# Attention's planned list begins with the last value group, holds the first output weights, and is planned anew (one Trainium2 core)

## The chip, the core and the metric

The kernel runs on one core of one Trainium2 chip. Five engines share the core's memory: TensorE (PE, matmuls; PEld are its weight loads), VectorE (DVE), ScalarE (ACT), GpSimd (POOL) and SyncE (SP, which issues the DMAs here). Each engine works off its own queue in order and waits at an instruction until what that instruction needs is there. The metric is the device time of one execution in microseconds (us); lower is better. Of the kernel before there are three runs, 1249.63 to 1252.88 us, median 1252.07 us.

## What is computed

One decoder layer on 1024 tokens of width 1024, in float32:

```python
h   = x * (1 + scale1) + shift1                  # modulation from c
q, k, v, u, iq, ik, iw = split(h @ w_in)         # 8 heads of 64; rope on q, k, iq, ik
score = sum_h iw_h * relu(iq_h . ik)             # the indexer, causal
keep the 256 highest scores of each query row; softmax attention over those alone
mixer = concat(attention, causal window pools of u) @ w_o
x = LayerNorm(alpha * x + gate1 * mixer)
x = LayerNorm(alpha * x + gate2 * SwiGLU(x * (1 + scale2) + shift2))
```

The choice of 256 keys a row is exact: the kernel searches a threshold for each row, bit by bit, and turns it into a mask that is added to the attention scores. Tokens are worked in eight tiles of 128 rows; tile i sees 128(i + 1) keys, so tiles 0 and 1 need no search.

## The kernel before, in words

**Matmuls.** A float32 operand is split into a high and a low part and multiplied in three passes (`SPLITS`), so a projection group of 128 tokens by 512 columns is 8 x 3 = 24 matmuls.

**Stages.** (1) Modulation and indexer projections. (2) Indexer scores. (3) Projection groups, the list `groups` (line 969): eight pooling groups, eight key groups, eight value groups, worked in the loop of lines 974 to 1021; actions that belong to a group are put off to a later slot with `at_`. Value group t is copied from its PSUM bank by `v_take` one slot later. (4) Attention, lines 1166 to 1392. (5) Output projection (`wo_*`) and the first LayerNorm, then the feed-forward part in a hand-made order, which the change does not touch.

**Threshold searches.** `bisect` (line 607) is a generator that yields one step at a time with the engine and an expected cost. There are streams for the tiles [3], [5, 4] (search passes on ACT, a `Sign` activation with a summed output), and [7, 6], [2] (on DVE; tile 2 drops the largest scores eight at a time, `drop_eights`, line 590). Each ends in `mask_steps`. During the projection groups, `fill` (line 727) slips a step in wherever the modelled queue has room. Line 975 appends to `hold` at the last value group: from there `fill` starts no step on ACT and none of a tile other than 7's stream.

**Attention's list.** Work is cut into 32 units (head pair pr, tile i), two of them making one output. A unit is a row of tasks, each with an engine, a cost and a rank: `s` scores on PE, `x` (mask, scale and row maximum, DVE), `e` exponentials (ACT), `r` reciprocal (DVE), `n` multiplication by it (POOL), `p` transposes (PE), `c` copies of these out of PSUM (ACT or DVE); then `o`, the product with the values (PE), `hi` (ACT) and `lo` (DVE). For each query tile below 6 there are `load` (SP), `turn` (PE transposes), `own` and `other` (ACT) and `low` (DVE) as well. PSUM banks are two rings (four small, two large). A list scheduler (lines 1356 to 1391) then repeats: it works out the earliest start of every task and search step that could go, takes all that could start within `SPAN` of the earliest, and emits the one of lowest rank (`PRIO`, for search steps `CHAIN_PRIO`; `V_BIAS` is added to the start of a copy on DVE). What it emits is the fixed program order on PE, DVE, ACT and POOL. So the costs decide only the order; the chip decides when each instruction runs.

**Before and after the list.** The last two groups' copies (`late` slots 24 and 25) come ahead of it. After it come, in the program, the output weights: `wo_load(k)` (DMA, then the gate row multiplied in on POOL) and `wo_split(k)` (high part on ACT, low part on DVE). These are not held in order, and the compiler's scheduler moves them up among the attention's instructions where it sees room. WO[0] and WO[1] lie where the rows of query tiles 7 and 6 lay; WO[2] to WO[7] lie where the keys lay. Three raw slots (`raw_slot`) take turns for query rows, output weights and pooled rows.

Of the kernel before, what the change touches and what calls it, by code (L numbers as in the profile page):

```python
# [18 lines left out]
ALU = mybir.AluOpType  # L19

P = 128
# [19 lines left out]
EAGER = 0  # L41
Q_LEAD = 40
CHAIN_LEAD = 1
V_BIAS = -0.075
SPAN = 0.106
PRIO = {'load': -387, 'turn': -49, 'own': -168, 'low': -13, 'other': -88, 's': 3, 'x': -36, 'e': 1, 'r': 152, 'n': -121, 'p': 12, 'c': 332, 'o': -134, 'hi': -115, 'lo': 145}
CHAIN_PRIO = {2: (500, 22.3), 3: (347, 6.4), 4: (-732, 10.2)}
AHEAD_SMALL = 2
NORM = 2
NORM_SMALL = 2  # L50
# [145 lines left out]
def decoder_layer_kernel(  # L196
# [375 lines left out]

    def mask_steps(i, T1, ng, eq, lt):
        n, sc, w = P * (i + 1), score(i), (i + 1) / 8
        yield "V", 1.7 * w + 0.1

        V.tensor_scalar(eq, sc, T1, None, ALU.is_equal)
        V.tensor_scalar(lt, sc, T1, float(TOPK - n), ALU.is_lt, ALU.add, accum_out=ng)
        V.tensor_scalar(ng, ng, -0.5, None, ALU.add)
        yield "V", 1.6 * w  # L580
        left = sc.bitcast(BF16)[:, 0:n]
        V.tensor_tensor_scan(left[:, ::-1], eq[:, ::-1], eq[:, ::-1], ng, ALU.add, ALU.bypass)
        V.tensor_scalar(left, left, 0.0, None, ALU.is_lt)
        yield "V", 1.8 * w
        V.tensor_tensor(eq, eq, left, ALU.mult)
        V.tensor_tensor(lt, lt, eq, ALU.max)
        V.tensor_scalar(sc, lt, NOT_TAKEN, None, ALU.mult)
        biased.add(i)

    def drop_eights(i, cols):  # L590

        n = P * (i + 1)
        neg = buf("X", 4800, n, "neg")
        m8, ng, T1 = cols[:, 0:8], cols[:, 8:9], cols[:, 9:10]
        yield "V", 0.5
        V.tensor_scalar(neg, score(i), -1.0, None, ALU.mult)
        for r in range((n - TOPK) // 8):
            yield "V", 1.0
            V.max(m8, neg)
            V.match_replace(neg, m8, neg, -3.4e38)  # L600
        yield "V", 0.7
        V.max(m8, neg)
        V.tensor_scalar(T1, m8[:, 0:1], -1.0, None, ALU.mult)
        halves = neg.bitcast(BF16)
        yield from mask_steps(i, T1, ng, halves[:, 0:n], halves[:, n : 2 * n])
# [365 lines left out]
    PAIRS = (0, 6, 8, 14, 16)  # L971
    held, pair = {}, None
    qr = {}
    for n_, (kind, a, b) in enumerate(groups):
        if n_ == len(groups) - 1:
            hold.append(1)
        if n_ == 17:
            qr.update((i, q_load(i)) for i in (7, 6))
        if n_ in (20, 21):
            at_(n_, lambda i=27 - n_: q_make(i, qr[i]))  # L980
        if n_ in PAIRS:
            pb = psB("pair")
# [12 lines left out]
        if n_ in (7, 8, 15, 16):  # L995
            for kp in ((0, 1) if n_ % 2 else (2, 3)):
                w_split(kp)
        nd = n_ + 2 if n_ in PAIRS else n_ + 1
        if kind == "u":
            at_(nd, lambda a=a, b=b, pp=pp: u_take(a, b, pp))  # L1000
            if b == 1:
                at_(nd + 1, lambda a=a: u_split(a))
                at_(nd + 1, lambda a=a: u_split2(a))
                at_(nd + POOL_AT, lambda a=a: u_pool(a))
        elif kind == "k":
            tr = n_ + (4 if n_ in PAIRS or n_ - 1 in PAIRS else 3)
            at_(nd, lambda a=a, pp=pp, tr=tr: take(a, pp, tr))
        else:
            at_(nd, lambda a=a, pp=pp: v_take(a, pp))
        if n_ == 20:  # L1010
            SP.dma_start(GR, gate_d[0].to_broadcast([P, 1024]))
        q_ = n_ - MOD_AT
        if 0 <= q_ < 9:
            if q_:
                mod_fin(q_ - 1)
            if q_ < 8:
                mod_half(2 * q_)
        for f in late.pop(n_, []):
            f()
        if 0 <= q_ < 8:  # L1020
            mod_half(2 * q_ + 1)
    last = len(groups)
    pinned.clear()


    stat = [buf("X", 8448, 128, "stat")]
# [6 lines left out]

    ptb = [[buf("H", (2 * s_ + e) * 2048, 2048, "pT").rearrange("p (j q) -> p j q", j=8) for e in (0, 1)] for s_ in (0, 1)]
    smr = buf("H", 8192, 6144, "sm")
    for s_ in (last, last + 1):
        for f in late.pop(s_, []):
            f()
    assert not late, late
    def cat_slot(g):  # L1040
        return WS[g]

# [79 lines left out]
    def wo_load(k):  # L1122
        wo_raw[k] = raw_slot()
        SP.dma_start(wo_raw[k], wo_in[k])
        G.tensor_tensor(wo_raw[k], wo_raw[k], GR, ALU.mult)

    def wo_split(k):
        split(WO[k], wo_raw[k], 1024)
# [10 lines left out]
    def pool_split(q):  # L1139
        r = pl_raw[q].rearrange("p (g t) -> p g t", t=256)  # L1140
        for hi, lo, src in ((PLT0[:, 0, q], PLT0[:, 1, q], r[:, 0]),
                            (PLT[:, ::-1, 0, q], PLT[:, ::-1, 1, q], r[:, 1:4])):
            A.activation(hi, src, AF.Copy)
            V.tensor_tensor(lo, src, f_(hi), ALU.subtract)

    class Task:

        def __init__(self, kind, q, cost, rank, emit, deps=(), slots="", late=0.0):
            self.q, self.cost, self.rank, self.emit, self.deps, self.slots, self.late = q, cost, rank + PRIO[kind], emit, deps, slots, late
            self.end, self.kind, self.masks = None, kind, ()  # L1150

    class Ring:

# [20 lines left out]
    sm_of, o = {}, 0  # L1174
    for u in units:
        n = P * (u[2] + 1)
        if n > 512:
# [6 lines left out]
    q_done, q_turns = {7: (), 6: ()}, []  # L1184
    masked = {0: 0.0, 1: 0.0}

    def q_rows(t, rank):
        hold_ = {}

# [22 lines left out]
                V.tensor_tensor(lv[64:128], pv[64:128], f_(qv[64:128, :, 1, :]), ALU.subtract)  # L1212

        l_ = task("load", "S", 0.1, rank, load, q_turns[-3:-2], late=4.0)
        t_ = task("turn", "T", 0.55, rank, turn, (l_,), "A", late=0.2)
        c0 = task("own", "A", 1.2, rank, lambda: copies(0), (t_,))
        lw = task("low", "V", 1.4, rank, lambda: copies(2), (c0,))
        c1 = task("other", "A", 1.2, rank, lambda: copies(1), (c0,))
        t_.readers = (c1, lw)
        t_.masks = {1: (3,), 0: (4, 5)}.get(t, ())  # L1220
        q_done[t] = (c1, lw)
        q_turns.append(t_)

    def unit(k):
# [18 lines left out]
        def n_(e):  # L1243
            G.tensor_scalar(sms[e], sms[e], cols["c"][:, 2 + e : 3 + e], 0.0, ALU.mult, ALU.add)

        s_t = task("s", "T", 0.2 + 0.0014 * n, 10 * k - EAGER, s_, q_done[i], "B" if n <= 512 else "BB", late=0.2)
        before = [t for w in where for t in sm_users.get(w, ())]
        xs = [task("x", "V", 0.08 + 0.00105 * n, 10 * k, lambda e=e: x_(e), [s_t] + before, late=0.12) for e in (0, 1)]
        for x in xs:
            x.masks = (i,)  # L1250
        s_t.readers = xs
# [4 lines left out]
        for e in (0, 1):  # L1256
            for j0 in range(0, i + 1, 4):
                m = min(4, i + 1 - j0)
                hold_ = {}

                def p_(e=e, j0=j0, m=m, hold_=hold_):
                    hold_["pt"] = pt = psA("pT")
                    for j in range(m):
                        T.transpose(pt[:, j * P : (j + 1) * P], sms[e][:, (j0 + j) * P : (j0 + j + 1) * P], ident)

# [9 lines left out]
                c = task("c", "AV", (0.09 + 0.11 * m, 0.09 + 0.13 * m), 10 * k + 3, c_, [p] + list(o_tasks[-2:-1]), late=0.1)  # L1275
                p.readers = (c,)
                ps.append(p)
                cs.append(c)
        for w in where:
            sm_users[w] = ps  # L1280
        return cs

    o_tasks = []
# [3 lines left out]
    for k in range(0, nu, 2):  # L1287
# [11 lines left out]
            ca = cat_slot(g)  # L1299
            V.tensor_tensor(ca[:, 1024 + pr * 256 : 1024 + (pr + 1) * 256], hold_["po"][:, 0:256], f_(ca[:, pr * 256 : (pr + 1) * 256]), ALU.subtract)  # L1300

        o_t = task("o", "T", 0.1 + 0.865 * (g + 1), 10 * k + 14, o_, cs, "A", late=0.3)
        h_t = task("hi", "A", 0.3, 10 * k + 15, hi_, (o_t,), late=0.1)
        l_t = task("lo", "V", 0.38, 10 * k + 16, lo_, (h_t,), late=0.1)
        o_t.readers = (l_t,)
# [1 line left out]
    class Chain:  # L1307
# [5 lines left out]
        def step(self):  # L1313
# [4 lines left out]
            self.cost = (0.95 if self.q == "A" else 1.08) * self.st[1][1]  # L1318
# [11 lines left out]
    def earliest(t, q):  # L1330
        at = clock[q]
        for d in t.deps:
            if d.end is None:
                return FAR
            at = max(at, d.end)
        for i in t.masks:
            if i not in masked:
                return FAR
# [23 lines left out]
    while todo or chains:  # L1362
# [15 lines left out]
        if q == "T":  # L1378
            cost += 0.15 * (kind[0] != t.kind)
            kind[0] = t.kind  # L1380
        if t.slots:
            t.got = rings[t.slots[0]].take(len(t.slots))
        t.emit(q) if len(t.q) > 1 else t.emit()
        clock[q] = at + cost
        t.end = at + cost + t.late
        todo.remove(t)
# [744 lines left out]
```

## Time and profile before

| | value |
|---|---|
| runs, median (range) | 1252.07 us (1249.63 to 1252.88) |
| profiled execution, its own time | 1250.99 us |
| span, first to last instruction | 1249.2 us |
| busy: PE / DVE / ACT / POOL | 1180.4 / 1002.0 / 656.0 / 709.3 us |
| mean granted TensorE clock | 0.981 |
| attention's list, first score matmul to last output matmul | about 333.7 to 472.3 us |

In the profile's answers a row of a timeline gives the start, the duration and the engine, then the tile written, the tiles read, the shape and the count of merged instructions; a bracket at its end gives the idle time of the engine ahead of it and what ended that. A row of the table by stretches gives, for each engine in turn (PE, PEld, DVE, ACT, POOL), the busy time and in brackets the number of instructions, then the granted TensorE clock (1.00 is full speed), the DMA share and GB/s. A row of groups gives total busy us, mean ns of one, and the idle time before them. All compute is emitted through one helper at line 183, so tiles are told apart by name: `s` scores, `sm` the weights of a unit, `pT` their transposes, `o` the output, `pj` a projection group, `qT` and `qab` a query tile turned and its copies, `vf` values, `keysA`, `junkB`, `colsA` the search of tile 3, `neg`, `colsE` that of tile 2, `raw` the raw slots, `wo` output weights and their product.

### The profile page before, as it was taken

To read this page: it belongs to the slowest core of one execution; us is meant where nothing else is said; L and a number is where in the kernel's file an instruction comes from. 1 tells how busy PE (TensorE), PEld (TensorE's weight loads), DVE (VectorE), ACT (ScalarE), POOL (GpSimd) and SP (SyncE) were. 2 spreads that over 40 slices of the span, in tenths; PEclk is the share of its full clock that TensorE was granted. 3 is DMA by queue.
4 is the path that set the end of the run, shared out by engine and by line. 5 is a ranking of instruction groups with operands and counts; after the bars stand their busy time and mean duration, and the time that the engine had idled before them with its cause. 6 is when DMAs were issued, how large, how long until landed. Compare 5 with 4: busy or idle time off the path is not lost.

```text
span 1249.2 us, 16310 instructions
## 1 busy us (share of the span) xinstructions
PE 1180.4 (94%) x5622; PEld 919.8 (74%) x5622; DVE 1002.0 (80%) x1772; ACT 656.0 (53%) x1330; POOL 709.3 (57%) x505
## 2 busy tenths in 40 slices
PE   8999989999888899997899999999999999999996
PEld 6756556687665568876778787877878787878775
DVE  6799997988989975686977878787777768687698
ACT  4667878787789683455343434333333333442521
POOL 0093484676034362286784838475665748486848
PEclk9999999999989899997999999999999999999998
DMA  9610167421101035001312111112102020213212
GB/s 349 251 49 11 47 242 280 154 70 60 43 1 35 34 134 174 39 9 34 102 34 68 34 68 34 68 34 67 68 34 72 32 99 23 81 34 101 68 51 118
DMA packets 32459, 103.40 MB, mean 83 GB/s; under 512 B 3572, under 2 KB 3572, under 8 KB 28792
## 3 DMA queue, kind: packets, MB, share of 16 engines
q1 hardware_dynamic: 32376, 102.36, 23.1%
q8 instruction: 44, 0.72, 0.2%
q14 instruction: 39, 0.32, 0.1%
HBM read 92.90 MB, written 9.45 MB: 82 GB/s over the span
## 4 chain that ended last, share of the span: by engine, by line
PE 38%; DVE 7%; POOL 5%; issue 2%; ACT 1%; DVEq 0%; POOLq 0%; ACTq 0%
PE gu L183 23%; PE dn L183 15%; DVE act_W L183 2%; DVE utmp_X L183 2%; POOL wraw_R L183 1%; POOL wblk_T L183 1%; POOL wraw_W L183 1%; POOL wblk_V L183 1%; DVE gtmp_V L183 1%; DVE wblk_T L183 1%; DVE hr_H L183 0%; POOL hr_H L183 0%; DVE stat_C L183 0%; DVE wblk_V L183 0%; DVE res_X L183 0%
## 5 line engine op out<-in xcount | busy, mean ns | idle before, releaser
L183 PE MATMUL gu<-hr_H,wblk_T 128*128 128x512 f32 (+1 forms) x924 | 216.9, 387 | 2.6 <-ACT gtmp_V L183 2.3
L183 PE MATMUL gu<-hr_H,wblk_V 128*128 128x512 f32 (+1 forms) x924 | 215.1, 384 | 2.4 <-ACT gtmp_V L183 1.7
L183 PEld LDWEIGHTS gu<-hr_H,wblk_T 128*128 128x128 f32 x924 | 171.7, 190 | 38.7 <-ACT gtmp_V L183 2.9
L183 PEld LDWEIGHTS gu<-hr_H,wblk_V 128*128 128x128 f32 x924 | 170.0, 188 | 38.6 <-ACT gtmp_V L183 2.2
L183 DVE TENSOR_TENSOR res_X<-res_X,dn 128x512 f32<-128x512 f32 (+1 forms) x253 | 158.5, 675 | 15.4 <-PE dn L183 15.3
L183 POOL TENSOR_TENSOR wraw_R<-wraw_R 128x512 f32<-128x512 f32 x64 | 93.9, 1475 | 45.8 <-DVE wblk_T L183 23.1
L183 POOL TENSOR_TENSOR wraw_W<-wraw_W 128x512 f32<-128x512 f32 x60 | 85.8, 1437 | 55.8 <-DVE wblk_V L183 27.4
L183 PE MATMUL pj<-ws_W,hT_H 128*128 128x512 f32 x456 | 115.7, 400 | 1.0 <-DVE ws_W L183 1.0
L183 POOL TENSOR_SCALAR sm_H<-sm_H,stat_X 128x1024 f32<-128x1024 f32 (+7 forms) x64 | 49.1, 783 | 96.9 <-DVE stat_X L183 83.0
L183 PEld LDWEIGHTS pj<-ws_W,hT_H 128*128 128x128 f32 x456 | 83.0, 188 | 24.9 <-issue 6.5
L183 PE MATMUL dn<-wblk_T,act_W 128*128 128x512 f32 x324 | 79.4, 393 | 1.9 <-POOL wblk_T L183 1.2
L183 PE MATMUL dn<-wblk_V,act_W 128*128 128x512 f32 x324 | 78.8, 392 | 1.1 <-POOL wblk_V L183 1.1
L183 DVE TENSOR_SCALAR_CACHE_REDUCE junk_X<-keysD_T,colsD_X 128x1024 int16<-128x1024 int16 (+1 forms) x64 | 79.4, 1268 | 0.2
L183 ACT ACTIVATE wblk_V<-wraw_R 128x512 fp32r<-128x512 f32 x56 | 35.2, 629 | 80.7 <-POOL wraw_R L183 69.1
L183 PEld LDWEIGHTS dn<-wblk_T,act_W 128*128 128x128 f32 x324 | 60.1, 188 | 17.4 <-POOL wblk_T L183 3.9
L183 ACT ACTIVATE wblk_V<-wraw_W 128x512 fp32r<-128x512 f32 x53 | 33.1, 628 | 75.9 <-POOL wraw_W L183 62.4
L183 PEld LDWEIGHTS dn<-wblk_V,act_W 128*128 128x128 f32 x324 | 60.2, 188 | 16.2 <-POOL wblk_V L183 3.9
L183 ACT ACTIVATE wblk_T<-wraw_W 128x512 fp32r<-128x512 f32 x56 | 35.0, 628 | 65.9 <-POOL wraw_W L183 53.8
L183 ACT ACTIVATE wblk_T<-wraw_R 128x512 fp32r<-128x512 f32 x52 | 32.5, 627 | 61.3 <-POOL wraw_R L183 51.3
L183 PE MATMUL pT<-const_C,sm_H 128*128 128x128 f32 x288 | 45.2, 299 | 15.7 <-POOL sm_H L183 8.2
L183 DVE SCALAR_TENSOR_TENSOR score_X<-relu_K,const_C,score_X 128x384 f32<-128x384 f32 (+5 forms) x42 | 54.1, 1289 | 5.0 <-ACT relu_K L183 1.3
L183 ACT ACTIVATE utmp_X<-gu 128x512 f32<-128x512 f32 x33 | 19.7, 598 | 73.0 <-PE gu L183 73.0
(301 smaller groups left out, 2717.4 us busy)
## 6 DMA issues: line engine op xcount, KB each, us to landing
mset_K<-in_wmr_dram SPq DMA_DIRECT2D x16, 1024.0 KB, 5.3
wm_K<-in_wma_dram SPq DMA_DIRECT2D x16, 512.0 KB, 10.2
wraw_R<-in_wg_dram SPq DMA_DIRECT2D x6, 1024.0 KB, 4.7
wraw_R<-in_wd_dram SPq DMA_DIRECT2D x12, 512.0 KB, 3.6
wraw_W<-in_wup_dram SPq DMA_DIRECT2D x12, 512.0 KB, 3.5
wraw_R<-in_wup_dram SPq DMA_DIRECT2D x10, 512.0 KB, 3.6
wraw_W<-in_wg_dram SPq DMA_DIRECT2D x5, 1024.0 KB, 4.8
wraw_W<-in_wd_dram SPq DMA_DIRECT2D x10, 512.0 KB, 3.5
```

The costliest lines, as they stand in the source:

```text
L183: ins_ = f(*a, **k)
```

## The change

1. The loop over `groups` leaves out the last value group. Its matmuls and the last two copies are tasks (`group`, `take`) of the list. What overwrites memory that this group reads waits for it: the query rows of tiles 5, 4 and 3, the rows `x` of every unit but the first, the first copies of a unit. The first unit gets rows of its own (`sm_first`), so it can run ahead of the group.
2. Nothing is put into `hold`, and the queues stay held in order from the groups into the list, SP too.
3. The output weights' first three loads and gate products and the first two splits are tasks of the list. Loads are issued in the order in which they were made (`behind`).
4. A one-column exponential is put at slot 22, so the table for exponentials is loaded there.
5. When the list expects PE to wait more than 0.5 us ahead of transposes, it puts spare transposes (0.55 of the gap less 0.5 us, 0.11 us each) into the bank first.
6. Costs of tasks are changed, some search steps get a separate cost for the list, and all ranks, `SPAN` and `V_BIAS` are new.

```diff
-V_BIAS = -0.075
-SPAN = 0.106
-PRIO = {'load': -387, 'turn': -49, 'own': -168, 'low': -13, 'other': -88, 's': 3, 'x': -36, 'e': 1, 'r': 152, 'n': -121, 'p': 12, 'c': 332, 'o': -134, 'hi': -115, 'lo': 145}
-CHAIN_PRIO = {2: (500, 22.3), 3: (347, 6.4), 4: (-732, 10.2)}
+V_BIAS = 0.15
+KEEP = 0.55
+SPAN = 0.15
+PRIO = {'load': 650, 'turn': 53, 'own': -1350, 'low': -687, 'other': 600, 's': -261, 'x': -1371, 'e': 71, 'r': -915, 'n': 1966, 'p': -227, 'c': 659, 'o': -951, 'hi': -1034, 'lo': 641, 'gate': -895, 'group': 863, 'take': 1269, 'whi': -1001, 'wlo': -635}
+CHAIN_PRIO = {2: (1157, 15.6), 3: (1224, 52.0), 4: (1044, 55.3)}
...
-        yield "V", 1.7 * w + 0.1
+        yield "V", 1.7 * w + 0.1, False, 1.7 * w + 0.5
...
-        yield "V", 1.6 * w
+        yield "V", 1.6 * w, False, 3.4 * w
...
-        yield "V", 1.8 * w
+        yield "V", 1.8 * w, False, 2.9 * w
...
-            yield "V", 1.0
+            yield "V", 1.24
...
-    for n_, (kind, a, b) in enumerate(groups):
-        if n_ == len(groups) - 1:
-            hold.append(1)
+    for n_, (kind, a, b) in enumerate(groups[:-1]):
...
+        if n_ == 22:
+            at_(n_, lambda: A.activation(colsE[:, 16:17], ident[:, 0:1], AF.Exp))
...
-    last = len(groups)
-    pinned.clear()
+    last = len(groups) - 1
...
-    for s_ in (last, last + 1):
-        for f in late.pop(s_, []):
-            f()
+    (take_22,) = late.pop(last)
...
+    sm_first = [buf("X", 5312, 1024, "sm"), buf("V", 7168, 1024, "sm")]
...
+    def group_23():
+        got["pp"] = psA("pj")
+        t_f(groups[-1][1])(got["pp"], range(KT))
+
+    vg = task("group", "T", 3.4, 0, group_23, (), "A", late=0.2)
+    va = task("take", "A", 0.55, 0, take_22, (), late=0.1)
+    vb = task("take", "A", 0.55, 0, lambda: v_take(groups[-1][1], got["pp"]), (vg,), late=0.1)
...
-        t_ = task("turn", "T", 0.55, rank, turn, (l_,), "A", late=0.2)
+        t_ = task("turn", "T", 0.55, rank, turn, (l_, vg) if t > 2 else (l_,), "A", late=0.2)
...
-        s_t = task("s", "T", 0.2 + 0.0014 * n, 10 * k - EAGER, s_, q_done[i], "B" if n <= 512 else "BB", late=0.2)
+        s_t = task("s", "T", 0.1 + 0.0014 * n, 10 * k - EAGER, s_, q_done[i], "B" if n <= 512 else "BB", late=0.2)
...
-        xs = [task("x", "V", 0.08 + 0.00105 * n, 10 * k, lambda e=e: x_(e), [s_t] + before, late=0.12) for e in (0, 1)]
+        xs = [task("x", "V", 0.08 + 0.00105 * n, 10 * k, lambda e=e: x_(e), [s_t] + before + [vg] * (k > 0), late=0.12) for e in (0, 1)]
...
+                    for _ in range(spare):
+                        T.transpose(pt[:, 0:P], ident, ident)
...
-        o_t = task("o", "T", 0.1 + 0.865 * (g + 1), 10 * k + 14, o_, cs, "A", late=0.3)
+        o_t = task("o", "T", 0.865 * (g + 1) - 0.1, 10 * k + 14, o_, cs + [va, vb] * (g == 3), "A", late=0.3)
...
+    for k in range(3):
+        d_ = task("load", "S", 0.1, 200, lambda k=k: wo_dma(k), (q_turns[3 + k],), late=5.0)
+        g_ = task("gate", "G", 2.35, 200 + k, lambda k=k: wo_gate(k), (d_,), late=0.15)
+        if k < 2:
+            h_ = task("whi", "A", 1.05, 205 + k, lambda k=k: wo_hi(k), [g_] + o_tasks[3:4], late=0.1)
+            task("wlo", "V", 1.15, 206 + k, lambda k=k: wo_lo(k), (h_,))
...
+        spare = 0
+        if t.kind == "p":
+            gap = at - max(clock[q], rings["A"].ready(1))
+            spare = max(0, int(KEEP * (gap - 0.5) / 0.11))
...
-    wo_load(0)
-    wo_split(0)
-    wo_load(1)
-    wo_load(2)
     times.fill = None
-    wo_split(1)
     wo_split(2)
     for k in range(3, KT):
```

More of the change, by code (lines that the diff above doesn't have):

```diff
@@ L1120, in decoder_layer_kernel, with wo_dma, wo_gate, wo_load @@
     wo_raw = {}
-    def wo_load(k):
+    def wo_dma(k):
         wo_raw[k] = raw_slot()
         SP.dma_start(wo_raw[k], wo_in[k])
+    def wo_gate(k):
         G.tensor_tensor(wo_raw[k], wo_raw[k], GR, ALU.mult)
+    def wo_load(k):
+        wo_dma(k)
+        wo_gate(k)
     def wo_split(k):
@@ L1144, in pool_split @@
             V.tensor_tensor(lo, src, f_(hi), ALU.subtract)
+    loads = []
     class Task:
@@ L1149, in __init__ @@
             self.q, self.cost, self.rank, self.emit, self.deps, self.slots, self.late = q, cost, rank + PRIO[kind], emit, deps, slots, late
-            self.end, self.kind, self.masks = None, kind, ()
+            self.end, self.kind, self.masks, self.behind = None, kind, (), loads[-1:] if kind == "load" else []
+            if kind == "load":
+                loads.append(self)
     class Ring:
@@ L1176, in decoder_layer_kernel @@
         n = P * (u[2] + 1)
-        if n > 512:
+        if u == units[0]:
+            sm_of[u] = sm_first, {6}
+        elif n > 512:
             sm_of[u] = [smr[:, (o + e) % 6 * 1024 :][:, 0:n] for e in (0, 1)], {o % 6, (o + 1) % 6}
@@ L1183, in decoder_layer_kernel @@
     sm_users, live = {}, {}
-    q_done, q_turns = {7: (), 6: ()}, []
+    q_done, q_turns, turns = {7: (), 6: ()}, [], {}
     masked = {0: 0.0, 1: 0.0}
+    got = {}
+    def group_23():
[4 more added lines that the diff above has]
+    vb = task("take", "A", 0.55, 0, lambda: v_take(groups[-1][1], got["pp"]), (vg,), late=0.1)
+    vg.readers = (vb,)
+    rings["A"].free[-1][0] = 1.0
     def q_rows(t, rank):
@@ L1259, in unit, with p_ @@
                 hold_ = {}
-                def p_(e=e, j0=j0, m=m, hold_=hold_):
+                def p_(spare=0, e=e, j0=j0, m=m, hold_=hold_):
                     hold_["pt"] = pt = psA("pT")
+                    for _ in range(spare):
+                        T.transpose(pt[:, 0:P], ident, ident)
                     for j in range(m):
@@ L1274, in unit @@
                 p = task("p", "T", 0.107 * m, 10 * k + 3, p_, (ns[e],), "A", late=0.25)
-                c = task("c", "AV", (0.09 + 0.11 * m, 0.09 + 0.13 * m), 10 * k + 3, c_, [p] + list(o_tasks[-2:-1]), late=0.1)
+                c = task("c", "AV", (0.09 + 0.11 * m, 0.09 + 0.13 * m), 10 * k + 3, c_, [p] + (list(o_tasks[-2:-1]) or [vg]), late=0.1)
                 p.readers = (c,)
@@ L1280, in unit @@
             sm_users[w] = ps
+        if k == 0:
+            turns[2].deps = list(turns[2].deps) + ps
         return cs
@@ L1317, in step, with wo_hi, wo_lo @@
             self.q = self.st[1][0]
-            self.cost = (0.95 if self.q == "A" else 1.08) * self.st[1][1]
+            self.cost = self.st[1][3] if len(self.st[1]) > 3 else (0.9 if self.q == "A" else 1.02) * self.st[1][1]
+    def wo_hi(k):
+        A.activation(WO[k][:, 0:1024], wo_raw[k], AF.Copy)
+    def wo_lo(k):
+        V.tensor_tensor(WO[k][:, 1024:2048], wo_raw[k], f_(WO[k][:, 0:1024]), ALU.subtract)
+    for k in range(3):
[4 more added lines that the diff above has]
+            task("wlo", "V", 1.15, 206 + k, lambda k=k: wo_lo(k), (h_,))
     t0 = T.t
@@ L1335, in earliest @@
             at = max(at, d.end)
+        if any(b.end is None for b in t.behind):
+            return FAR
         for i in t.masks:
@@ L1380, in decoder_layer_kernel @@
             kind[0] = t.kind
+        spare = 0
+        if t.kind == "p":
+            gap = at - max(clock[q], rings["A"].ready(1))
+            spare = max(0, int(KEEP * (gap - 0.5) / 0.11))
         if t.slots:
             t.got = rings[t.slots[0]].take(len(t.slots))
-        t.emit(q) if len(t.q) > 1 else t.emit()
+        if spare:
+            t.emit(spare)
+        else:
+            t.emit(q) if len(t.q) > 1 else t.emit()
         clock[q] = at + cost
```

1 line of the change is left out of this document (added).

## The prediction, on record before the change was run

> **What bounds the kernel now.** I read the page's 40 slices first, to find where PE is not full, then the busy times by stretch around the attention, then the timelines of PE, ACT and DVE there, and last the groups. The table by stretches (columns: stretch, its length, PE, PEld, DVE, ACT, POOL, granted clock) says which engine is full:
>
> ```profile
> 326.00:333.50 7.50, 7.50 (x35) 6.21 (x34) 7.21 (x13) 3.43 (x7) 0.00 (x0) 1.00 0.00 0
> 333.50:360.00 26.50, 19.61 (x96) 13.45 (x94) 22.05 (x46) 23.74 (x46) 6.42 (x6) 0.81 0.09 30
> 360.00:440.00 80.00, 69.59 (x489) 47.74 (x488) 74.37 (x183) 64.47 (x152) 36.41 (x33) 0.94 0.08 27
> 440.00:478.00 38.00, 37.78 (x276) 27.08 (x277) 25.70 (x89) 27.24 (x85) 18.03 (x31) 1.00 0.40 140
> ```
>
> The reader should see three regimes. The last groups fill PE. The list's start (333.5 to 360) fills nobody: PE idles 26.5 - 19.61 = 6.9 us, DVE 4.45, ACT 2.8, and the clock falls to 0.81. The middle is DVE's: 74.37 of 80 us, PE idle 10.4. From 440 PE is full again, with 0.2 us idle. So only 333.5 to 440 can give time, and there DVE, with 4.45 + 5.63 = 10.1 us idle, sets the ceiling.
>
> PE's timeline at the two ends of the list:
>
> ```profile
> 322.69 11.18 PE L183 MATMUL pj<-ws_W,hT_H 128*128 128x512 f32 x48
> 333.71 1.73 PE L183 MATMUL s<-kr_K,qab_V 128*128 128x512 f32 x8
> ...
> 342.60 1.11 PE L183 MATMUL pT<-const_C,sm_H 128*128 128x128 f32 x4 [2.84 <-POOL sm_H L183]
> 343.37 3.21 PE L183 MATMUL s<-kr_K,qab_V 128*128 128x512 f32 x8
> ...
> 472.26 6.87 PE L183 MATMUL wo<-wo_V,ws_W 128*128 128x512 f32 x29
> 478.96 8.32 PE L183 MATMUL wo<-hr_H,ws_W 128*128 128x512 f32 x36
> ```
>
> The last two value groups take 11.18 us, 5.6 each, back to back. Then the first unit's scores wait 342.60 - 333.71 = 8.9 us for their transposes. ACT's timeline shows why it is so long:
>
> ```profile
> 328.40 1.09 ACT L183 ACTIVATE vf_V<-pj 128x512 f32<-128x512 f32 x2
> 333.91 0.60 ACT L183 ACTIVATE vf_V<-pj 128x512 f32<-128x512 f32 x1 [4.42 <-PE pj L183]
> ...
> 337.38 1.28 ACT L183 ACT_TABLE_LOAD   x1
> 338.67 1.15 ACT L183 ACTIVATE sm_H<-sm_H,stat_X 128x1024 f32<-128x1024 f32 x1
> ...
> 354.06 0.71 ACT L183 ACTIVATE junkB_X<-keysA_X,colsA_X 128x512 bf16<-128x512 uint16 x1
> ```
>
> ACT idled 4.42 us under the last group, because `hold` keeps the search of tile 3 from it, and then loaded a table for 1.28 us with the first exponential waiting.
>
> **The change, part by part.** Gains count as minus.
>
> *The last group inside the list.* PE's next work after value group 6 ends at about 328.3 (322.69 + half of 11.18) is now the first unit's scores. The group (5.6 us) then lies under that unit's maximum, exponentials, reciprocal and multiplication. `x` of the second unit must wait for the group, but that comes after it anyway. The first transposes could start 8.9 - 1.28 = 7.6 us after 328.3, at 335.9, if PE were free; it has 1.73 + 5.6 us of scores and group to do, till 335.6, and likely the second unit's scores (1.73) ahead of them: 337 or so instead of 342.6. PE thus gains 5 us. But DVE's work is only moved: what it can win is its idle time, 4.45 us in the ramp and 0.3 under the last group. Bounds 0 (DVE fills up with search steps that it has to do at any rate, and idles later instead) to 5.6 (the whole group hidden). I take -3.5: three quarters of DVE's idle time there, since each of the gaps in that ramp was a wait of one engine for another.
>
> *Without `hold`, ACT has the 4.42 us for three passes of tile 3's search.* That search still had this to do:
>
> ```profile
> L183 ACT ACTIVATE pT_H<-pT 128x512 f32<-128x512 f32 (+3 forms) x30 | 14.5, 525 | 6.1 <-PE pT L183 6.1
> L183 ACT ACTIVATE junkB_X<-keysA_X,colsA_X 128x512 bf16<-128x512 uint16 x14 | 10.1, 719 | 1.5 <-DVE colsE_X L183 1.1
> L183 ACT ACTIVATE colsA_X<-colsA_X 128x1 f32<-128x1 f32 x28 | 8.2, 292 | 0.7
> L183 DVE COPY pT_H<-pT 128x512 f32<-128x512 f32 (+3 forms) x31 | 16.8, 578 | 0.2 <-PE pT L183 0.2
> L183 DVE MAX8 colsE_X<-neg_X 128x8 f32<-128x384 f32 x17 | 9.4, 552 | 1.5 <-ACT junkB_X L183 1.4
> L183 DVE MATCH_REPLACE8 neg_X<-colsE_X,neg_X 128x384 f32<-128x384 f32 x16 | 8.7, 543 | 0.0
> ```
>
> (ACT's and DVE's groups from 333.5 to 440.) A pass is 0.72 + 2 x 0.29 us and a short read, about 1.5 us, 14 in all. It makes room on ACT, which is not the bound; it is counted in the next term.
>
> *Copies pass from DVE to ACT.* `V_BIAS` goes from -0.075 to 0.15, so a copy goes to ACT unless DVE could start it 0.15 us sooner. From 333.5 to 440 DVE did 31 at 0.578 us and ACT 30 at 0.525. ACT has 80 - 64.47 = 15.5 us idle from 360 to 440, so it can take six more (3.2 us); DVE sheds 6 x 0.578 = 3.5 us of the work that bounds the middle. PE can follow, with 10.4 us idle. Bounds: 0, and 5.6 + 3.5 if DVE's idle time in the middle went as well. I take -3.0; a new order need not lower the idle time, since the order before was also the planner's.
>
> *The table load at slot 22.* It falls where ACT waits anyway (the 4.42 us); the 1.28 us on the first unit's path is inside the 7.6 above, so it is not added again. If the search's `Sign` needed another table, loads would alternate; but the pass at 354.06 runs after the load of 337.38 with none between. The Trainium skill ("ScalarE: Activation LUTs", What ACT_TABLE_LOAD costs) puts a further drain of about 1.38 us beside each load. Here the exponential starts at 338.67, right where the load ends, so the trace does not show it; by the page the first unit would gain 1.38 us more and the sum, ruled by DVE, would stay.
>
> *Spare transposes and the clock.* Scores that take 1.73 us at 333.71 take 3.21 at 343.37, after the 2.84 us gap. In clock terms 333.5 to 360 lost 0.19 x 26.5 = 5.0 us of PE time and the middle 0.06 x 80 = 4.8, mostly under DVE's work. Do transposes alone bring the clock back? From 353.87 PE does nothing but 26 transposes for 4.70 us:
>
> ```profile
> 354.00:356.00 2.00, 2.00 (x13) 1.99 (x13) 1.39 (x4) 1.98 (x6) 1.59 (x2) 0.61 0.00 0
> 356.00:358.00 2.00, 2.00 (x12) 2.00 (x11) 2.00 (x4) 1.69 (x3) 0.00 (x0) 0.54 0.00 0
> 358.00:360.00 2.00, 2.00 (x14) 1.26 (x11) 2.00 (x7) 1.98 (x6) 0.00 (x0) 1.00 0.00 0
> ```
>
> They do: 0.54, then 1.00. Bounds +1 (a spare row delays real ones where the list's gap is not the chip's) to -3. I take -1.0. The Trainium skill ("TensorE: Matmul & The Clock Gate", Part 4) says that the full clock does not engage for transposes. The rows above speak against it; by the page this term would be 0.
>
> *The output weights in the list.* Loads, gates and splits keep their number; PE has 0.2 us idle from 440 to 478 and goes from `o` straight into `wo`, so earlier weights buy nothing: 0. The gates' place matters on DVE, though:
>
> ```profile
> 417.14 2.37 POOL L183 TENSOR_TENSOR raw_R<-raw_R,gr_G 128x1024 f32<-128x1024 f32 x1 [2.92 <-PE pT L183]
> 417.35 2.44 DVE L183 TENSOR_TENSOR keysA_X<-keysA_X,score_X 128x512 bf16<-128x512 bf16 x1
> ...
> 419.83 0.43 DVE L183 TENSOR_TENSOR junkB_X<-junkB_X,keysA_X 128x512 bf16<-128x512 bf16 x1
> ```
>
> The same shape takes 0.43 us alone and 2.44 beside a gate: 2.0 us lost for each such meeting. One fewer or one more is as likely: 0, bounds ±2. A gate (rank -695) also beats a unit's multiplication (1966 and up) on POOL's queue when both could start; transposes queued on PE would then wait up to 2.37 us. Three gates: 0 to +7; POOL is under half full in the middle, so few meet. I take +0.5. SP is now held in order too; behind a weight load that waits for its slot stand only later weight loads, which PE wants after 468 at the earliest: 0.
>
> *A cost that is off.* The group is planned at 3.4 us and takes 5.6. What the list puts right behind it on PE comes 2.2 us later than planned, and DVE and ACT, in fixed order, can stand behind an `x` or a copy for that long, once. Bounds 0 to +2.2; I take +0.5.
>
> **Sum:** -3.5 - 3.0 - 1.0 + 0.5 + 0.5 = -6.5 us on the profiled execution's 1250.99 (span 1249.2): 1244.5. That execution lies 1.1 us below the median of the runs, 1252.07, so as a median 1245.6. All that follows the attention keeps its order and starts from its end, so nothing takes the gain back. A measurement here can tell about 0.3%, 3.8 us, from no change.
>
> **The rivals.**
>
> *No change (0.17).* DVE is the bound, its work is all still there, and a new list idles as long. For it: 96.42 us of DVE work in the 106.5 from 333.5 to 440. Against: the copies that leave DVE. What stays is about half of the shed copies, -1.5: 1250.6.
>
> *All of it (0.15).* DVE's 10.1 us of idle time go but for 1, and copies worth 3.5 leave: -12.6, 1239.5. For it: PE's work is short of DVE's, so nobody else is in the way. Against: each unit passes through four engines in turn, and the same kind of list left DVE 5.63 us idle in the 80 of the middle.
>
> *Slower (0.13): the searches come due.* Search steps now rank from 1157 and 1224 up and rise 15.6 and 52 a step, below every task of a unit but the multiplications, so they run where an engine has nothing else. Units 16 and 17 need masks 3 and 2. Before, they were just in time:
>
> ```profile
> 432.76 0.95 DVE L183 TENSOR_SCALAR score_X<-neg_X 128x384 f32<-128x384 bf16 x1
> 433.75 0.69 DVE L183 CUSTOM_DVE_ANT_0 sm_H<-s,score_X 128x512 f32<-128x512 f32 x1
> ```
>
> The mask's last step ended and the row maximum of unit 16 followed at once. A round of tile 2 costs 0.552 + 0.543 us and a short load, about 1.2 us, 16 in all. If n rounds are left when PE has run out of earlier units, 1.2n us stand alone. The 6.5 us are gone at n = 5.4; at n = 10 the time is 1245.6 + 12 = 1257.6. Against it: the list is work-conserving, and with ACT's and DVE's ramp gaps open the steps have more room early.
>
> *The forecast (0.55)* has a spread of its own of some ±4 us, mostly faster by over 0.3% (nine tenths of it). Faster: 0.55 x 0.9 + 0.15 = 0.65; slower 0.12 (nearly all of its case); the rest, 0.23, the same. The range leaves out most of the slower case and the tail of the best: 1237 to 1254.
>
> **What would show it.** Right: the group's 24 matmuls between the first unit's scores and its transposes, first transposes near 337, no table load there; DVE above 95% busy from its start to 430; DVE with some 25 copies where it had 31; PE full from about 433; `o` ending 6 to 7 us earlier. Wrong: PE idle ahead of unit 16 with DVE or ACT in search steps (the slower rival); a ramp as empty as before with POOL or ACT as releaser; or a DVE just as full and the attention as long (no change). If `o` ends early and the whole time does not follow, my claim about what comes after is wrong.

## The result, and the profile after

The changed kernel takes 1241.03 us (median of five runs, 1239.33 to 1243.05), 0.9915 of the kernel before (1252.07, by now of five runs too), with a 95% interval of 0.9898 to 0.9932. That is 11.0 us less. Timed once more beside later experiments it gave 0.9928 (0.9912 to 0.9943). The profiled execution took 1239.33 us, with a span of 1237.5. Busy times are now PE 1174.4, DVE 992.5, ACT 661.1 and POOL 707.9 us, and the mean granted clock is 0.987.

To place the gain I measure the list from the end of value group 6, where the two programs begin to differ, to the start of the output product's unbroken run on PE. These are the rows of the table by stretches (columns as in the prediction), before and then after:

```profile
328.30:472.30 144.00, 126.49 (x857) 87.83 (x855) 123.25 (x320) 113.39 (x281) 60.86 (x69) 0.93 0.15 54
```

```profile
326.70:459.60 132.90, 122.31 (x865) 84.93 (x863) 114.21 (x309) 120.20 (x298) 59.72 (x69) 0.97 0.17 58
```

The list is 144.00 - 132.90 = 11.1 us shorter, which is all of the gain. (Value group 6 itself ends 1.6 us earlier in this execution. Up to there the programs differ by no more than the early exponential, and the kernels below that keep the order of the kernel after end the group between 326.6 and 329.5.) DVE's work fell by 9.0 us, although two of tile 5's mask steps (0.56 us each) lie inside the measured stretch only after the change; its idle time (length less busy) fell only from 20.75 to 18.69. ACT took on 6.8 us. Here is the kernel after in the prediction's stretches:

```profile
326.00:333.50 7.50, 7.50 (x34) 5.68 (x34) 7.18 (x14) 7.24 (x16) 0.00 (x0) 1.00 0.00 0
333.50:360.00 26.50, 20.54 (x126) 13.51 (x125) 23.79 (x51) 24.00 (x46) 9.31 (x9) 0.94 0.10 30
360.00:440.00 80.00, 75.98 (x557) 53.16 (x557) 72.48 (x202) 74.05 (x185) 37.22 (x41) 0.98 0.11 37
440.00:478.00 38.00, 37.39 (x235) 28.42 (x234) 23.12 (x58) 24.22 (x68) 18.32 (x23) 1.00 0.51 178
```

The ramp, 333.5 to 360, is still open: PE idles 6.0 us there where it idled 6.9, though its clock is better, 0.94 for 0.81. In the middle PE is busy 75.98 where it was 69.59, and ACT, not DVE, is now the fullest of the two that feed it (74.05 against 72.48). PE's timeline shows the group in its new place, and the list's end:

```profile
326.73 1.73 PE L184 MATMUL s<-kr_K,qab_V 128*128 128x512 f32 x8
328.39 5.74 PE L184 MATMUL pj<-ws_W,hT_H 128*128 128x512 f32 x24
...
338.55 1.09 PE L184 MATMUL pT<-const_C,sm_X 128*128 128x128 f32 x8 [0.39 <-POOL sm_X L184]
...
345.11 0.63 PE L184 MATMUL pT<-const_C,sm_V 128*128 128x128 f32 x4 [3.25 <-issue]
...
459.57 7.09 PE L184 MATMUL wo<-wo_V,ws_W 128*128 128x512 f32 x30
466.50 8.32 PE L184 MATMUL wo<-hr_H,ws_W 128*128 128x512 f32 x36
```

The group lies between the first unit's scores and its transposes. These start at 338.55, 4.1 us earlier than before, and are followed by a new gap of 3.25 us, for which the trace names no releaser. DVE's and ACT's groups in the list (total us, mean ns) show what DVE shed:

```profile
L184 DVE COPY pT_H<-pT 128x512 f32<-128x512 f32 (+3 forms) x31 | 15.7, 541 | 0.2 <-PE pT L184 0.2
L184 DVE TENSOR_TENSOR keysA_X<-keysA_X,score_X 128x512 bf16<-128x512 bf16 x1 | 0.4, 416 | 0.0
L184 DVE TENSOR_TENSOR neg_X<-neg_X,score_X 128x384 bf16<-128x384 bf16 x1 | 0.3, 347 | 0.0
L184 DVE TENSOR_SCALAR score_X<-neg_X 128x384 f32<-128x384 bf16 x1 | 0.4, 363 | 0.0
L184 ACT ACTIVATE pT_H<-pT 128x512 f32<-128x512 f32 (+3 forms) x65 | 27.8, 491 | 1.1 <-PE pT L184 0.8
```

Over the whole list DVE copies 31 banks; before, it was

```profile
L183 DVE COPY pT_H<-pT 128x512 f32<-128x512 f32 (+3 forms) x45 | 23.5, 554 | 2.4 <-PE pT L183 2.4
```

so 14 copies and 23.5 - 15.7 = 7.8 us went to ACT. The mask multiplication that had met a gate on POOL takes 0.416 us, not 2.44.

### The profile page after: what moved, and what is told of

Read it like the earlier page. It is cut to its first block, busy times and chain, and to the rows that moved or that the text cites. A ratio compares the mean times of both kernels' runs of the same rounds, so it can differ in the third digit from the quotient of the medians.

```text
span 1237.5 us, 16332 instructions
## 1 busy us (share of the span) xinstructions
PE 1174.4 (95%) x5631; PEld 915.6 (74%) x5631; DVE 992.5 (80%) x1758; ACT 661.1 (53%) x1345; POOL 707.9 (57%) x505
## 4 chain that ended last, share of the span: by engine, by line
PE 38%; DVE 7%; POOL 5%; issue 2%; ACT 1%; DVEq 0%; POOLq 0%; ACTq 0%
PE gu L184 23%; PE dn L184 15%; DVE act_W L184 2%; DVE utmp_X L184 2%; POOL wraw_R L184 1%; POOL wblk_T L184 1%; POOL wraw_W L184 1%; POOL wblk_V L184 1%; DVE gtmp_V L184 1%; DVE wblk_T L184 1%; DVE hr_H L184 0%; POOL hr_H L184 0%; DVE stat_C L184 0%; DVE wblk_V L184 0%; DVE res_X L184 0%
## 5 line engine op out<-in xcount | busy, mean ns | idle before, releaser
L184 POOL TENSOR_SCALAR sm_H<-sm_H,stat_X 128x896 f32<-128x896 f32 (+7 forms) x62 | 45.8, 754 | 44.0 <-DVE stat_X L184 25.7
L184 ACT ACTIVATE junkA_T<-keys_T,colsA_X 128x768 bf16<-128x768 uint16 (+3 forms) x62 | 54.4, 877 | 3.8 <-DVE colsA_X L184 2.9
```

The costliest lines, as they stand in the source:

```text
L184: ins_ = f(*a, **k)
```

## The experiments

The first theory was that the gain is DVE's work: the 14 copies (7.8 us) and the mask steps that no longer run beside POOL's work (four rows, 5.9 us before and 1.5 after: 4.4 us). Its rivals were the group's 5.6 us hidden under the first unit, and the order as such. To change one thing and leave the rest, most kernels here have the list frozen: the scheduler's choices are written out as a string `SEQ`, in which a number is a task, `c4` a search step of tile 4's stream, and a letter behind a copy the engine that does it. Unedited, such a list is the kernel before or after, instruction for instruction.

Two measures are given for each: the ratio to the kernel before timed beside it, and the list's length in the profiled execution. The second shows where time went, but it is one execution, and two executions of the kernel after differ by 2.4 us in it:

> The kernel after, unchanged, as a measure for the three beside it. Both theories: ratio 0.9915 to the kernel before, about 1241, and a list that takes about 133 us from the end of value group 6 to the output product's unbroken run.

It came out at 0.9928, with this list:

```profile
326.85:462.11 135.26, 123.61 (x863) 85.96 (x863) 113.69 (x308) 119.97 (x297) 59.94 (x69) 0.96 0.17 57
```

So the kernel after stands for 133 to 135 us of list and for 0.9915 to 0.9928. A row is only told from it when it lies clearly outside both.

**copies_back.** Fourteen of ACT's copies go back to DVE, for instance 46 and 77:

```diff
-69 45 12 70 47 71 54 84 42V 55 72 44V c2 56 57 46A 59 85 61 48A
+69 45 12 70 47 71 54 84 42V 55 72 44V c2 56 57 46V 59 85 61 48A
...
-75 76 78 64A 104 65 77A 79A 105 106
+75 76 78 64A 104 65 77V 79A 105 106
```

> The kernel after with its list frozen in the order it has, and 14 of ScalarE's 65 pT_H copies, evenly spread over the list, done by VectorE at the same places: 45 on VectorE, 51 on ScalarE, as before the change; all else stays. Theory 1 (the gain is work taken off VectorE: 14 copies, 7.8 us of its busy time, and mask steps that no longer run beside GpSimd's weight multiplications): slower than the kernel after by 5 to 8 us, 1246 to 1249. Theory 2 (the gain is the last value group's 5.6 us under the first unit): slower by 0 to 2, since VectorE's end isn't what sets the list's. Theory 3 (the order as such): 0 to 3.

Measured: 0.9940 (0.9920 to 0.9961), 1244.02 us.

```profile
328.84:465.01 136.17, 124.01 (x864) 85.57 (x863) 118.22 (x320) 114.97 (x282) 59.72 (x69) 0.96 0.17 57
```

DVE has some 4.3 us more to do than in the two executions of the kernel after (118.22 against 114.0), and the list is 1 to 3 us longer; the ratio's interval still holds the kernel after. That is below what theory 1 asked: here DVE's work doesn't turn into time one for one.

**group_first.** The group (0) and its copies (1, 2) go ahead of the first unit's scores (33):

```diff
-33 3 8 c4 c3 13 1 c3 0 34 c3 c3 35 36 37 c4 49 2 38 c2 c3 39 4
+0 33 3 8 c4 c3 13 1 c3 c4 2 c2 c3 c3 34 35 36 37 49 38 c3 39 4
```

> The kernel after with its list frozen, and the last value group and its copy moved ahead of the first unit's score products, where it stood before the change; all else in the order of the kernel after. Theory 2: slower than after by 4.0 to 5.6 us (1245 to 1246.6), the group's 5.74 us of TensorE time standing open again. Theory 1: slower by at most 2, since VectorE still has the fewer copies and the clear mask steps, though the idle time at its start comes back in part. With both causes at their full size (7.8 + 4.2 + 5.6 is more than the 11.0 found) one of the three has to fall short.

Measured: 0.9931 (0.9909 to 0.9954), 1242.84 us.

```profile
326.58:462.39 135.81, 122.49 (x865) 85.79 (x863) 114.78 (x309) 120.21 (x298) 59.70 (x69) 0.96 0.17 57
```

Theory 2's 4.0 to 5.6 us do not show. The group's 5.74 us stand open again, and the list is 0.5 to 3 us longer, but neither measure is told from the kernel after. From 326 to 360 DVE was idle 34 - 29.27 = 4.7 us before, 3.0 in the kernel after and 4.0 here:

```profile
326.00:360.00 34.00, 27.12 (x151) 19.10 (x150) 29.97 (x61) 29.56 (x58) 7.73 (x8) 0.90 0.08 24
```

**copies_over.** The same number of copies the other way, in the order of the kernel before:

```diff
-42 50 67 68 13 81 69 51 39V 52 14 70 41V 53 43V 44 c3 71
+42 50 67 68 13 81 69 51 39A 52 14 70 41V 53 43V 44 c3 71
...
-61V 100 85 74V 76V 78A 86
+61A 100 85 74V 76V 78A 86
```

> The kernel before with its list frozen in the order it had, and 14 of VectorE's 45 pT_H copies, evenly spread, done by ScalarE in place: 31 and 65, as after the change. Theory 1: faster than before by 4 to 7.8 us (1244 to 1248). Theory 2: 0 to 2 faster, since the same order can't start later work earlier unless VectorE is what each step waits for. Theory 3 (the order): no change, because a copy that goes to ScalarE in the old order comes later than it did on VectorE.

Measured: 0.9998 (0.9982 to 1.0015).

```profile
328.15:471.29 143.14, 124.00 (x858) 84.17 (x856) 116.12 (x306) 118.28 (x295) 60.62 (x69) 0.96 0.16 54
```

This is the plainest blow to theory 1. DVE lost 7.1 us of work (123.25 to 116.12) and gained 6.3 us of idle time (20.75 to 27.02). Each x, copy and search step stands at its old place in DVE's queue, and its waits for ACT grew from some 14 to 19 us. The edit is not quite clean: the gates fell a little otherwise, and the two mask multiplications beside them took 1.67 and 0.34 us where they took 2.44 and 1.54. So some 2 us of the lost work are not the copies', and still nothing was gained.

**gates_moved.** The order of the kernel before, with the loads, gates and first split of the output weights placed in the list; gates 2 and 1 follow the mask multiplications that they had met:

```diff
-163 19 186 18 160A 187 165 162A 178 164A 188 180
+g0 163 19 186 18 160A 187 165 162A 178 164A h0 188 180
...
-254 275 261 251A 239 262 253A 255V c2 263 264 276
+254 275 261 251A 239 262 253A 255V c2 263 g2 264 276
...
-292 293 279 23 294 310 295 280 c2 281 273 322 311 282 283
+292 293 279 23 294 310 295 280 c2 281 273 322 311 282 g1 283
```

> The kernel before with its list frozen, and GpSimd's multiplications of the output weights 0, 3, 2 and 1 placed in that list at about their old times, but those of weights 2 and 1 after the mask multiplications of the units that they met (the 2.44 us and the 1.54 and 0.95 us ones), so that these should take about 0.42, 0.35 and 0.36. Nothing else is moved. Theory 1: faster than before by 3 to 4 us (1248 to 1249). If waits on VectorE's own results take up the time that the mask steps give back: 0 to 1.

Measured: 0.9979 (0.9964 to 0.9994), 2.6 us less.

```profile
328.04:468.81 140.77, 124.30 (x857) 85.11 (x855) 120.16 (x320) 112.69 (x281) 59.72 (x69) 0.95 0.17 55
```

Here DVE's shed work turns into time, as far as two executions can tell: 3.1 us less work, 3.2 us less list. The difference from copies_over, as I read it, is that no other engine takes it on. What remains of the meetings are two steps beside normalisations, 0.94 and 0.95 us.

**copies_gates.** Both edits together, in the order of the kernel before.

> The kernel before with its list frozen, the 14 copies on ScalarE as in copies_over and the four multiplications as in gates_moved, both together. Theory A (each part stands by itself; a copy pays only in an order that was laid out for it): faster than before by what the two gave alone, 3 to 4 us. Theory B (with the mask steps clear VectorE is still the engine that everything waits for, and the copies then pay): 6 to 9.

Measured: 1.0004 (0.9991 to 1.0017). Both theories fail: the copies cost 3.1 us (give or take 2.5) of what the gates had won, and nothing is left of it.

```profile
327.55:470.05 142.50, 125.50 (x857) 86.92 (x856) 115.92 (x309) 119.46 (x297) 60.70 (x69) 0.94 0.16 55
```

DVE does as little as in group_first (115.92 and 114.78 us) and ACT as much (119.46 and 120.21). The group stands ahead of the scores in both, and the large mask step is clear in both (0.426 and 0.416 us). Yet this list takes 142.5 us and that one 135.8: DVE idles 26.6 us here and 21.0 there. What differs is mostly the order; nine spare transposes, the early table load and two mask steps beside normalisations differ as well.

**both_back.** The edits of copies_back and group_first together, in the order of the kernel after.

> The kernel after with its list frozen, the 14 copies back on VectorE and the last value group back ahead of the first unit, together. Theory A: slower than the kernel after by the sum of the two, 5 to 6.5 us, so that about 4.5 to 6 of the 11 are left (the multiplications' places, 3, and the new order and the rest, 1.5 to 3). Theory B (the group's cover and the shed copies are the same VectorE time, each pays only what the other leaves): 3 to 4.

Measured: 0.9959 (0.9947 to 0.9971), 3.9 us (give or take 2.5) slower than the kernel after beside it.

```profile
328.46:464.66 136.20, 123.36 (x869) 86.05 (x867) 119.15 (x321) 115.42 (x282) 59.72 (x69) 0.97 0.17 57
```

It lies at theory B's 3 to 4; with this uncertainty theory A's 5 to 6.5 is not ruled out. With 45 copies on DVE and the group ahead, as in gates_moved, the list is 4.6 us shorter than there (136.20 against 140.77), and the time 2.5 us (give or take 2.4).

**weights_out.** The order of the kernel after without the ten weight tasks (529 to 538), and the old code after the list:

```diff
-281 29 529 294 274V c2 20 275 c3 295 30 296 282
+281 29 294 274V c2 20 275 c3 295 30 296 282
...
     pinned.clear()
+    wo_load(0)
+    wo_split(0)
+    wo_load(1)
+    wo_load(2)
     times.fill = None
+    wo_split(1)
     wo_split(2)
```

> The kernel after with its list frozen, but the ten weight tasks taken out of it and the output weights loaded, multiplied and split after the list's record, as before the change; the last group, the copies and the order of all else stay. Theory A (what the held weights bring is only where GpSimd's multiplications fall): as after, 0 to 1, if they fall clear of the mask multiplications, and slower by 2 to 4 if one or two meet them again. Theory C (the held loads bring a gain of their own, the weights being ready earlier): slower by 1 to 4 with the mask steps at 0.35 to 0.42 all the same.

Measured: 0.9958 (0.9944 to 0.9971), 3.8 us (give or take 2.6) slower than the kernel after beside it.

```profile
329.48:467.33 137.85, 125.31 (x863) 87.46 (x862) 116.68 (x306) 118.97 (x295) 61.70 (x69) 0.95 0.16 56
```

The meeting is back. First POOL's timeline, then DVE's:

```profile
424.69 2.39 POOL L184 TENSOR_TENSOR raw_R<-raw_R,gr_G 128x1024 f32<-128x1024 f32 x1
```

```profile
425.18 2.18 DVE L184 TENSOR_TENSOR keysA_X<-keysA_X,score_X 128x512 bf16<-128x512 bf16 x1
```

DVE's instruction ends at 427.36, 0.28 us after the gate (427.08). In the kernel before it ended at 419.79, 0.28 us after that gate (417.14 + 2.37). In copies_over it ended at 419.29, 0.27 us after a gate that ended at 419.02. So it isn't slowed by a factor; it stands until the gate is through. The Trainium skill ("SBUF — State Buffer", SBUF: two separate sides) says so: a DVE instruction with two SBUF inputs and a GpSimd instruction that reads SBUF take one port pair by an exclusive lock for the whole instruction, and the loser blocks. The rows agree. The price of a meeting is then the rest of the gate, up to 2.4 us. Theory A's condition and its size are met, but the meeting explains only 1.8 of the 3.8 us; how the rest splits between the places of the other gates, a gain of the held loads' own (theory C) and the noise stays open.

**bias_before.** The kernel before with one number changed, and planned anew:

```diff
-V_BIAS = -0.075
+V_BIAS = 0.15
```

> The kernel before with one number changed, V_BIAS from -0.075 to 0.15 as in the change, and its list planned anew: 33 of the pT_H copies on VectorE where 45 stood. All else (last group first, weights after the list, ranks, costs) stays. Theory A (a shed copy pays where the planner laid the order out for it): faster than before by 2 to 4 us. Theory D (a copy on ScalarE only moves the wait from VectorE to ScalarE, in any order; what copies_back lost came from putting copies where the order wasn't made for them): 0 to 1, or slower, with VectorE's waits for ScalarE grown by what its copies shrank.

Measured: 1.0039 (1.0024 to 1.0053), 1255.83 us: slower.

```profile
328.16:476.27 148.11, 129.49 (x856) 89.48 (x854) 117.40 (x311) 119.45 (x295) 59.61 (x69) 0.91 0.16 52
```

Theory D, and worse than it said. DVE's work is down 5.9 us and its idle time up 10 (20.75 to 30.71), its waits for ACT from some 14 to 20. The stretch where it goes:

```profile
400.00:420.00 20.00, 18.41 (x143) 12.94 (x139) 14.47 (x43) 19.58 (x55) 10.10 (x11) 1.00 0.07 25
420.00:440.00 20.00, 15.02 (x70) 9.29 (x70) 18.98 (x43) 14.15 (x35) 8.26 (x5) 0.74 0.25 79
```

ACT is full first, with DVE waiting (14.47 of 20); then DVE, with ACT and PE waiting, and PE's clock falls to 0.74. Twelve copies moved off DVE helped neither. How much of the longer list is the clock's is not separated.

**old_ranks.** The kernel after with the old ranks, `SPAN` and `V_BIAS`, planned anew (43 copies on DVE):

```diff
-V_BIAS = 0.15
+V_BIAS = -0.075
...
-SPAN = 0.15
+SPAN = 0.106
...
-CHAIN_PRIO = {2: (1157, 15.6), 3: (1224, 52.0), 4: (1044, 55.3)}
+CHAIN_PRIO = {2: (500, 22.3), 3: (347, 6.4), 4: (-732, 10.2)}
```

> The kernel after with the old PRIO, CHAIN_PRIO, SPAN and V_BIAS (the new kinds of task at rank 0), planned anew: last group in the list, weights held, costs as in the change, exponential table loaded ahead; 43 copies on VectorE. Theory A (parts: group 1 to 2, copies 2 to 3, the weights' places 3 to 4, the new order 1 to 2): slower than after by 3 to 5 us, 1244 to 1246, if its multiplications miss the mask steps, and by 6 to 8 if two meet them. Theory E (the ranks as such are the gain): slower by 8 or more with no multiplication meeting a mask step.

Measured: 0.9952 (0.9939 to 0.9965), 1244.94 us.

```profile
328.15:465.16 137.01, 126.26 (x857) 86.88 (x855) 119.59 (x318) 113.05 (x284) 59.60 (x69) 0.94 0.16 57
```

The time is as theory A expected: 6.0 us of the gain are there with the old ranks, and the kernel after has some 3 to 5 more. Theory E falls. But the parts are not those of theory A, for with the old ranks the planner puts the last group ahead of the first unit again, as PE's timeline shows:

```profile
322.71 11.18 PE L184 MATMUL pj<-ws_W,hT_H 128*128 128x512 f32 x48
333.73 1.73 PE L184 MATMUL s<-kr_K,qab_V 128*128 128x512 f32 x8
...
350.50 1.97 PE L184 MATMUL pT<-const_C,sm_X 128*128 128x128 f32 x8
```

So these 6.0 us hold no cover for the group and only two of the 14 copies, and the first transposes start 7.9 us later than before the change, with a list 7.0 us shorter: the start of the first transposes does not set the list's end. both_back has the new ranks, the group ahead and 45 copies, and stands at the same place (0.9959 and 136.20 us against 0.9952 and 137.01). DVE idles 17.4 us here and 17.1 there, and 20.6 in gates_moved, which keeps the old plan. What planning anew brings beyond the gates' places is thus there with either set of ranks; what the new ranks add is where the group and 12 copies go.

**no_table.** The kernel after, frozen, without the early exponential:

```diff
-        if n_ == 22:
-            at_(n_, lambda: A.activation(colsE[:, 16:17], ident[:, 0:1], AF.Exp))
```

> The kernel after with its list frozen, without the early one-element exponential: the table's load falls into the first unit's exponentials again. If the load counts in full: slower by 1.3 us. If ScalarE's idle time around the first exponential hides it, or the first unit's start doesn't set the list's end: 0.

Measured: 0.9912 (0.9895 to 0.9929), list 132.19 us: no difference. ACT's timeline:

```profile
331.96 1.28 ACT L184 ACT_TABLE_LOAD   x1
334.60 1.15 ACT L184 ACTIVATE sm_X<-sm_X,stat_X 128x1024 f32<-128x1024 f32 x1 [1.36 <-DVE stat_X L184]
```

The load ran while the exponential still waited for the row maximum. It is hidden because it doesn't wait for what the exponential waits for.

**gate_and_x.** An attempt at a better version: unit 0's x (34, 35) ahead of tile 4's mask steps, and gate 3, which ran at 424.18 ahead of waiting normalisations, held behind task 374:

```diff
-33 3 8 c4 c3 13 1 c3 0 34 c3 c3 35 36 37 c4 49 2 38 c2 c3 39 4
+33 3 8 34 35 c3 13 1 c3 0 c3 36 c4 37 c4 38 c3 49 2 c2 c3 39 4
...
-381 348 371 357 533 537 25 372 394 358 334V 359 350 336V 382 373 395 337 383 374 396
+381 348 371 357 d3 533 537 25 372 394 358 334V 359 350 336V 382 373 395 337 383 374 g3 396
```

> The kernel after with its list frozen and two places changed: unit 0's score passes on VectorE ahead of tile 4's first two mask steps (score passes from about 331.4 where 333.4), and the multiplication of output weight 3, which ran at 424 ahead of eight waiting normalisations, held in the list behind the four of 384 columns (about 430). Theory A (VectorE's waits in 326 to 440 are what is left): faster than after by 1 to 3 us. If the list's end is set by VectorE's and ScalarE's busy time alone: 0.

Measured: 0.9910 (0.9895 to 0.9924), 1239.45 us, list 132.21: the lowest median of all, but not told apart from the kernel after. The x did start at 331.57 instead of 333.37, yet DVE's timeline shows why it bought nothing:

```profile
331.57 1.22 DVE L184 CUSTOM_DVE_ANT_0 sm_X<-s,score_X 128x1024 f32<-128x1024 f32 x1
...
333.86 1.55 DVE L184 TENSOR_TENSOR_SCAN score_X<-keys_T,colsA_X 128x640 bf16<-128x640 bf16 x1
...
337.26 0.16 DVE L184 RECIPROCAL stat_X<-stat_X 128x2 f32<-128x2 f32 x1
```

The unit's reciprocal still stands behind the mask steps, and the transposes start at 338.69. Gate 3's new place did shorten DVE's wait for the x of 512 columns that follows (0.18 us at 428.19, where the two executions of the kernel after have 1.00 and 2.65), but that gives no gain that can be told either.

Not tried by themselves: the spare transposes, the changed costs, the list without `hold`, and SP held in order.

## Why the prediction was right, and where it was not

The forecast, 1245.6 us and faster, had the right sign and place, and the result lies in its range; the size was 11.0 us where it said 6.5. Two kernels between make a path on which each step is measured: before to gates_moved -2.6 us (give or take 1.9), from there to both_back -2.5 (give or take 2.4: the new plan, with group and number of copies as they were), from there to after -3.9 (give or take 2.5: copies and group together). They add up to 9.0, the kernel after by its later timing (0.9928), and not to the 11.0 of the first.

Put beside the sum, copies and group together gave 3.9 us where 6.5 were forecast, the gates gave 2.6 where the sum had +0.5, and the new plan gave 2.5 that the sum had no term for. That the total lies in the range is in part luck: two terms too large stand against two gains that were not seen.

*The output weights in the list* is the term that failed. It said "One fewer or one more is as likely: 0, bounds ±2" and added 0.5. The kernel before had two gates beside mask steps, one that cost 2.0 us and a second that cost 1.2 on its first multiplication, and the list after has none: -2.6 by gates_moved, and -3.8 by weights_out, of which one meeting explains 1.8. The rows for the first were quoted; those of the second, from POOL's timeline and then DVE's, are

```profile
429.14 2.39 POOL L183 TENSOR_TENSOR raw_R<-raw_R,gr_G 128x1024 f32<-128x1024 f32 x1 [5.91 <-issue]
```

```profile
430.21 1.54 DVE L183 TENSOR_TENSOR neg_X<-neg_X,score_X 128x384 bf16<-128x384 bf16 x1
```

where the same shape takes 0.35 us after the change. The step to take was to count both meetings as a loss that a new list more likely lowers than raises: no cost in the plan stood for them, so they were there by chance.

*The last group:* -3.5 was too much. Undone alone it is worth 0.5 to 3 us of list and 1.2 us of time, with an uncertainty of about 3, so it is not told from nothing. Its working, that DVE can win no more than its idle time in the ramp, fits; three quarters of it does not. From 326 to 360 that idle time fell only from 4.7 to 3.0 us. DVE's queue had tile 4's mask steps and part of a query tile ahead of the first unit's x, from 328.46, when the scores were ready, to 333.37, so the unit started later than the working has it.

*Copies:* -3.0 is about what undoing them costs (1 to 3 us of list, 2.4 ± 3 of time), but that is luck: the working, copies times 0.578 us, is not how they act. Three kernels move such copies in the structure of before and gain nothing or lose. As I read them, a copy pays only where ACT's turn comes as early as DVE's would have, and that the whole order decides. Of the window 333.5 to 440 the prediction said 25 copies on DVE, and 25 it was; the other eight of the 14 left DVE outside it.

*Table load* 0: right, though for a better reason than the one given. *The cost that is off:* not seen by itself. *Spares and clock,* -1.0: spares are put in only once, nine of them. The clock did rise, from 0.93 to 0.97 in the list, but old_ranks has 0.94 and most of the gain, and copies_over has 0.96 and none, so it is not shown to be a cause.

*What should have shown it:* transposes near 337 (338.55), no load there, and o ending 6 to 7 us earlier (11). "DVE above 95% busy from its start to 430" is wrong: from 326 to 440 it idles 10.5 us, as it did before (10.4). DVE does not become fuller; it has less to do. The rival of searches that come due did not cost anything new. PE does idle 2.2 us from 416 to 422, while DVE ends tile 3's mask, and the first x of 512 columns follows at once, at 422.02; but from 412 to 422 of the kernel before, beside tile 3's mask, PE idled 3.0.

What stays open is how copies and group share their 3.9 us, and what in planning anew brings the 2.5: it is not the ranks as such, since old_ranks has it too, and not the early table load; the changed costs, the missing `hold` and SP's order were not run by themselves.

## What to carry to other kernels

When two engines share the work of a fixed order and both are busy for most of it (here 86% and 79%), a piece moved from one to the other at its place in the order can become a wait: measure the order as a whole, not pieces times price. Work that vanishes (a stall on a shared port) came back here at about its full length on the engine that bounds. Before costing a change of plan, list every stall of the old plan that came about by chance; both new plans that hold the weights (the kernel after and old_ranks) had lost the two meetings with gates.

## What the runs showed of the hardware

A table load starts while the exponential behind it waits for its semaphore (331.96 against 334.60), so loading a table ahead is worth nothing where ACT idles 1.28 us before the first use. A two-input bf16 multiplication on DVE that began beside a gate's multiplication on POOL ended 0.27 or 0.28 us after it, three times, where it takes 0.42 us alone. And one program's list differs from execution to execution (132.9 and 135.3 us). Up to DVE's mask multiplication at 420.6 the two executions of the kernel after run alike within 0.1 us. From 428 to 436 PE is busy throughout in both, but at a granted clock of 1.00 in the first and 0.57 in the second, with 54 matmuls done in the one and 32 in the other:

```profile
428.00:436.00 8.00, 8.00 (x54) 5.16 (x54) 6.83 (x25) 7.74 (x22) 6.11 (x10) 1.00 0.37 134
```

```profile
428.00:436.00 8.00, 8.00 (x32) 5.55 (x31) 3.41 (x12) 4.65 (x13) 4.66 (x8) 0.57 0.11 24
```

A product with the values then starts at 433.52 in the first and at 436.38 in the second, 2.9 us later. The first execution has its low clock earlier, 0.50 from 422 to 424, and loses less by it. So a difference of 2 to 3 us between two single executions can come from the clock; what decides where it falls is not shown.
